# The small products for 1/rms and weight stand in one row in every group of experts

## The chip, the cores and the metric

The kernel runs on one core of one Trainium2 chip. The metric is the device time of one execution in microseconds (us); less is better. TensorE (PE in the rows) multiplies, VectorE (DVE), ScalarE (ACT) and GpSimd (POOL) work element by element, and SyncE (SP) issues all transfers from HBM in one queue.

## What is computed

A block of two models on 256 tokens of 1024 features: sparse attention, a mixture of experts, a gated embedding, a second attention with a second mixture of experts and gated embedding, and then a feed-forward part, a mixer and another feed-forward part. The change touches the two mixtures alone. Cut to what matters:

```python
def hier_moe(xn, w_group, b_group, w_expert, b_expert, w_gate, w_up, w_down):
    ...
    e_w, e_idx = lax.top_k(e_prob, TOPK_IN_GROUP)     # 2 of 8 experts in one of 4 groups
    e_w = e_w / jnp.sum(e_w, axis=-1, keepdims=True)
    comb = g_w * e_w
    ...
    hid = jax.nn.silu(jnp.einsum('td,edf->tef', xt, w_gate)) * jnp.einsum('td,edf->tef', xt, w_up)
    y = jnp.einsum('tef,efd->td', hid * cw[:, :, None], w_down)
```

Each token goes to 2 of 32 experts (`w_gate`, `w_up`: 1024 x 128 each, `w_down`: 128 x 1024). The input `xn` is normalised, so each token has a factor 1/rms as well as its two weights.

## The kernel before

The experts are worked through in four groups of eight (`gq` 0 to 3). Each expert has 32 slots, so a group has 256 slots, in two halves of 128 (`pp` 0 and 1; a half is four experts). For a group the kernel does this:

- `slots` (L1018 and after, on VectorE): for each of two tiles of tokens `t` it makes matrices of zeros and ones that say which token sits in which slot: `G1[t][:, 0]` for a token's first expert, `G[:, t]` for both. `slots_second` makes `G1[t][:, 1]`, for the second expert (on GpSimd in groups 1 to 3).
- `gather` (L1063, TensorE): 32 products with `G` bring the tokens into slots, each with a moving operand of 256 columns over the whole 128 x 128 array.
- `gate_up` (L1086, TensorE): for each half 32 products, called with `u` 0 to 3, eight each. A product uses 32 columns of the array (`128*32` in the rows), and the four experts `x` of a half use the four groups of 32 columns, so that four products can be under way side by side. In the trace each of these fp32 products is two instructions; a half is therefore 64.
- `slot_values` (L1044, TensorE): eight small products with `G1` as the stationary 128 x 128 operand and four moving columns `rw` (1/rms and weight of each token, each in two parts). They give each slot its 1/rms and weight in a PSUM tile. VectorE then makes `sv` (L1049) and `rr` (L1053, L1054) of it. The function is a generator: each `next` issues one product, the ninth issues the VectorE part.
- `finish` (L1117 to L1132): SiLU with `rr`, the down product L1128, scaling with `sv`. `combine` (L1234) adds the result to the tokens. The last group's own version of these is `last_group` (down products L1175).

In groups 0 to 2 the small products are issued by `gate_up` of the second half, one after every second product of it (`x % K["svx"] == 0`, with `svx` 2):

```python
if beside and x % K["svx"] == 0:
    next(beside, None)
```

In group 3 `last_group` begins with `list(values)`, which issues all eight at once. What follows a half's products in groups 0 to 2 is `slots` of the next group, which writes into the two `G1` buffers that the small products of this group read (the pool has two), and then its `gather`.

Loads: the gate and up weights (`in_moe_gu`, 1 MB each, L282) and the down weights (`in_moe_dn`, 512 KB each, tile `wd`, L1102) are issued on SP's queue as soon as the buffers that they go to were read by the products of an earlier group. A scheduler with priorities decides the order of instructions on each engine. In the second mixture one expert has more tokens than slots, and a branch after `combine` of group 1 works through it as a whole (L1418 to L1477); in the first the branch is passed over.

Of the kernel before, what the change touches and what calls it, by code (L numbers as in the profile page):

```python
# [23 lines left out]
K = dict(  # L24
    raw=9,
    e=7,
    w4=5,
    load_at=[1, 1],
    over_at=1,
    defer=0,  # L30
    kinds='rwwrererrrrwrr',
    mid='e',
# [17 lines left out]
    split_first=1,  # L50
    w1_early=1,
    sv=1,
    svx=2,
    fill={'nsa:0': [2, 0], 'nsa:3': [3], 'ffn:0': [6, 7], 'mixer:0': [12, 13], 'ffn:2': [16], 'moba:3': [8, 4], 'nsa:5': [5], 'ffn0:2': [17, 15], 'nsa:2': [9, 14, 1], 'nsa:7': [10], 'ffn0:3': [11]})
FF_GROUPS = [4, 4, 4, 4, 4, 2]
Z_WIDTHS = [512, 512, 304, 256, 512, 512]
# [140 lines left out]
class Block:  # L197
# [63 lines left out]
    def inline(self, ins, line="tail"):  # L261

        self.tc.stamp_issue_order_token(ins.ins, line)
        return ins
# [699 lines left out]
    def moe(self, i, aT, w_out):  # L964
# [9 lines left out]
        def pump(kind):  # L974

            if hold:
                held.append(kind)
            elif pending:
                load(*pending.pop(0), dict(r="raw", e="e", w="w4")[kind])
# [92 lines left out]
        def gather(gq, k):  # L1072
            ps = self.psb([P, 2, 256])
            for t in range(2):
                gather_tile(gq, k, ps, t)

        def gate_up(gq, pp, u, beside=None, bank=None):
            _, _, xg, pgs, _ = st[gq]
            if u == 0:
                pgs.append((bank or self.psa)([P, 2, P]))  # L1080
            where, wg = ahead.pop((gq, pp, u))
            for kk in range(2):
                k = 2 * u + kk
                for x in range(4):
                    o = pp * P + 32 * x
                    mm = nc.tensor.matmul(pgs[pp][32 * x:32 * x + 32], xg[:, k, o:o + 32], wg[kk][:, x],  # L1086
                                          start=(k == 0), stop=(k == KT - 1))
                    if gq == 3 and pp:
                        inline(mm)
                    if beside and x % K["svx"] == 0:  # L1090
                        next(beside, None)
            if where == "raw" and kept and (gq, pp, u) >= kept[0]:
                kept.clear()
            elif where == "raw" or where == "e" and K["recycle"]:
                pump(where[0])
# [87 lines left out]
        def combine_half(back, n):  # L1183
            for t in range(2):
                ps = self.psa([P, 512])
                for b, (GT, y) in enumerate(back):
                    inline(nc.tensor.matmul(ps, GT[:, t * P:(t + 1) * P], y[:, n * 512:(n + 1) * 512],  # L1187
                                            start=(b == 0), stop=(b == len(back) - 1)))
                inline(self.add_h(n, t, ps))

        def last_group(back, values):

            list(values)
            first_hidden = hidden(3, 0)
            next(first_hidden)
            gate_up(3, 1, 0, None, self.psb)
            gate_up(3, 1, 1)
            hT = next(first_hidden)
            combine_half(back, 0)
            gate_up(3, 1, 2)  # L1200
            combine_half(back, 1)
            GT = [token_parts(pp) for pp in range(2)]
            gate_up(3, 1, 3)
            y = [down_products(3, 0, wd[3, 0], hT)]
            self.fine = bool(K["fine"])
            self.gate_first = [list(self.halves(self.unit("w_gate", i * D * D, 2048), 2048, 4))]
            second_hidden = hidden(3, 1)
            next(second_hidden)
            acc = [[self.psa([P, 512]) for _ in range(2)] for _ in range(2)]

            def gathered(pp, n, t):
                for part in range(2):
                    inline(nc.tensor.matmul(acc[t][n], GT[pp][:, t * P:(t + 1) * P], y[pp][part][:, n * 512:(n + 1) * 512],
                                            start=(pp + part == 0), stop=(pp + part == 2)))

            with self.ahead_by("finish"):
                for n in range(2):
                    gathered(0, n, 0)
                hT = next(second_hidden)
                for n in range(2):  # L1220
                    gathered(0, n, 1)
                y.append(down_products(3, 1, wd[3, 1], hT))
                for t in range(2):
                    for n in range(2):
                        gathered(1, n, t)
                        inline(self.add_h(n, t, acc[t][n]))
# [34 lines left out]
        def load_down(gq, pp):  # L1261
            wd[gq, pp] = weights_down(8 * i + 2 * gq + pp)
# [59 lines left out]
        def point(gq, j):  # L1322
            if not K["defer"] and [gq, j] == list(K["load_at"]):
                over_n.append(self.overflow_load(i, n_full, first))

        for gq in range(4):
            if K["defer"] and gq == K["over_at"]:
                hold.append(1)
            values = slot_values(gq)
            if gq == 3:  # L1330
                last_group(back, values)
                break
            if K["svx"] == 0:
                list(values)
            point(gq, 0)
            for u in range(4):
                gate_up(gq, 1, u, values if K["svx"] else None)
            list(values)
            point(gq, 1)
            slots_start(gq + 1)  # L1340
            slots(gq + 1)
            for k in range(4):
                gather(gq + 1, k)
            back = finish(gq, 0, wd[gq, 0])
            if not hold:
                load_down(gq + 1, 0)
            for u in range(4):
                gate_up(gq + 1, 0, u)
            back = back + finish(gq, 1, wd[gq, 1])
            point(gq, 2)  # L1350
            if not hold:
                load_down(gq + 1, 1)
            point(gq, 3)
            if gq == 2:
                continue
            combine(back)
            if gq == K["over_at"]:
                if K["defer"]:
                    over_n.append(self.overflow_load(i, n_full, first, False))
                self.overflow(i, xh, r, w, OH, over, full, over_n[0], first, xT if K["keep"][i] else None)  # L1360
                if not hold:
                    pump("r")
                if hold:
                    hold.clear()
                    for kind in held[:4]:
                        pump(kind)
                    if gq < 3:
                        for pp in range(2):
                            load_down(gq + 1, pp)
                    for kind in held[4:]:  # L1370
                        pump(kind)
# [425 lines left out]
```

## Time and profile before

| | |
|---|---|
| median of 3 runs | 1105.34 us (1105.32 to 1106.97) |
| the profiled execution | 1107.02 us, of which the span of its instructions 1105.0 us |
| mean granted TensorE clock | 0.985 of full |
| busy: PE, DVE, ACT, POOL | 1056.6, 688.9, 517.9, 21.5 us |
| moved by DMA | 268.53 MB, mean 243 GB/s |

The span is the time from the first to the last instruction of the profiled execution. All times in rows count from its start. The first mixture lies at about 205 to 315 us, the second at about 445 to 572 us. A column `PEclk` of 1.00 is the full clock of TensorE (2.4 GHz), 0.5 is the half (1.2 GHz); a value between is a stretch with both.

### The profile page before, as it was taken

The page shows a single profiled execution, that of the slowest core. Times are in us where ns is not written, and L with a number is a line of the kernel's source. Part 1 is how long each engine was busy: PE and PEld are TensorE (multiplying, and loading weights), DVE is VectorE, ACT ScalarE, POOL GpSimd, SP SyncE. Part 2 cuts the span into 40 slices and gives each one's busy share as a digit, 9 for nine tenths or more (in the row PEclk, how much of TensorE's full clock was granted, in tenths as well). Part 3 has the DMA queues.
Part 4 walks back from the last instruction along what each step waited for, and adds up shares of the span by engine and source line. Part 5 has one row for each costly group of instructions (what it writes and reads, how often), then busy time and mean ns, then how long its engine had stood idle before and what let it go on. Part 6 is the DMA issues. An engine that isn't in the chain of part 4 may idle for free.

```text
span 1105.0 us, 18061 instructions
## 1 busy us (share of the span) xinstructions
PE 1056.6 (96%) x6941; PEld 819.6 (74%) x6941; DVE 688.9 (62%) x1730; ACT 517.9 (47%) x1015; POOL 21.5 (2%) x31
## 2 busy tenths in 40 slices
PE   7999999899999999999998999999989989999996
PEld 5885556765557657667556899899969768999995
DVE  6687684643478954644368756565684876555555
ACT  5356575222267675123156543443554755444442
POOL 2000000000100000000000000000000000000000
PEclk9998999899999999899999999999999999999999
DMA  9664568689994485799797656755574354554401
GB/s 371 277 232 193 239 252 324 242 309 383 415 416 174 168 336 182 276 350 380 279 390 279 251 188 210 287 190 181 211 317 178 121 223 153 190 191 153 144 29 38
DMA packets 46506, 268.53 MB, mean 243 GB/s; under 512 B 5328, under 2 KB 7120, under 8 KB 20432
## 3 DMA queue, kind: packets, MB, share of 16 engines
q1 hardware_dynamic: 46416, 267.34, 64.0%
q8 instruction: 56, 0.92, 0.3%
q14 instruction: 34, 0.28, 0.1%
HBM read 266.27 MB, written 1.05 MB: 242 GB/s over the span
## 4 chain that ended last, share of the span: by engine, by line
PE 46%; DVE 3%; ACT 1%; issue 1%; DVEq 0%
PE b L312 7%; PE b L313 7%; PE b L314 7%; PE a L312 6%; PE a L313 6%; PE a L314 6%; PE a L1086 1%; DVE lo L300 1%; PE b L1568 1%; DVE w L1590 1%; DVE h L1591 0%; PE b L1063 0%; PE a L1187 0%; ACT hi L299 0%; DVE nq L327 0%
## 5 line engine op out<-in xcount | busy, mean ns | idle before, releaser
L300 DVE TENSOR_TENSOR lo<-raw,hi 128x1024 fp32r<-128x1024 f32 (+2 forms) x234 | 271.6, 1164 | 189.2 <-ACT hi L299 184.8
L299 ACT ACTIVATE hi<-raw 128x1024 fp32r<-128x1024 f32 (+2 forms) x234 | 235.6, 1011 | 253.1 <-PE b L313 125.6
L312 PE MATMUL a<-hi,e 128*128 128x512 f32 (+2 forms) x576 | 225.2, 392 | 2.5 <-ACT e L399 1.7
L313 PE MATMUL a<-lo,e 128*128 128x512 f32 (+2 forms) x576 | 223.0, 388 | 0.9 <-DVE lo L300 0.9
L314 PE MATMUL a<-hi,e 128*128 128x512 f32 (+2 forms) x576 | 223.0, 388 | 0.0
L312 PE MATMUL b<-e,hi 128*128 128x256 f32 x640 | 181.5, 284 | 0.0
L313 PE MATMUL b<-e,hi 128*128 128x256 f32 x640 | 181.1, 283 | 0.0
L314 PE MATMUL b<-e,lo 128*128 128x256 f32 x640 | 180.9, 283 | 0.0
L312 PEld LDWEIGHTS a<-hi,e 128*128 128x128 f32 x576 | 109.2, 190 | 25.3 <-ACT e L399 2.8
L313 PEld LDWEIGHTS a<-lo,e 128*128 128x128 f32 x576 | 109.1, 189 | 22.6 <-DVE lo L300 2.1
L314 PEld LDWEIGHTS a<-hi,e 128*128 128x128 f32 x576 | 108.7, 189 | 22.0 <-DVE e L389 0.4
L312 PEld LDWEIGHTS b<-e,hi 128*128 128x128 f32 x640 | 122.8, 192 | 1.1 <-ACT hi L299 0.8
L313 PEld LDWEIGHTS b<-e,hi 128*128 128x128 f32 x640 | 122.8, 192 | 0.3
L314 PEld LDWEIGHTS b<-e,lo 128*128 128x128 f32 x640 | 122.8, 192 | 0.0
L1086 PE MATMUL a<-raw,e 128*32 128x256 f32 x704 | 66.1, 387 | 1.1 <-DVEq L1404 0.8
L591 ACT ACTIVATE p<-p,m 128x128 f32<-128x128 f32 (+1 forms) x96 | 42.8, 449 | 13.4 <-DVE m L586 11.4
L336 ACT ACTIVATE junk<-h 128x512 bf16<-128x512 f32 x40 | 25.4, 643 | 37.5 <-DVE h L496 21.9
L1086 PEld LDWEIGHTS a<-raw,e 128*32 128x32 f32 x704 | 27.5, 110 | 15.1 <-issue 2.5
L1063 PE MATMUL b<-G,e 128*128 128x256 f32 x224 | 35.8, 307 | 2.4 <-DVE e L1246 2.3
L586 DVE CUSTOM_DVE_ANT_0 p<-a,consts 128x128 f32<-128x128 f32 (+1 forms) x96 | 31.8, 350 | 10.0 <-PE a L579 3.2
L496 DVE TENSOR_TENSOR h<-h,a 128x512 f32<-128x512 f32 x40 | 26.8, 685 | 16.3 <-PE a L1187 6.6
L269 ACT ACTIVATE e<-b,small 128x256 f32<-128x256 f32 x32 | 15.2, 476 | 44.4 <-DVE e L271 44.2
(339 smaller groups left out, 1373.1 us busy)
## 6 DMA issues: line engine op xcount, KB each, us to landing
raw<-in_ffn SPq DMA_DIRECT2D x62, 1024.0 KB, 4.8
raw<-in_moe_gu SPq DMA_DIRECT2D x52, 1024.0 KB, 7.6
raw<-in_w_ada SPq DMA_DIRECT2D x36, 1024.0 KB, 5.8
wd<-in_moe_dn SPq DMA_DIRECT2D x64, 512.0 KB, 7.1
raw<-in_w_gate SPq DMA_DIRECT2D x8, 1024.0 KB, 13.0
raw<-in_w_m_in SPq DMA_DIRECT2D x8, 1024.0 KB, 6.3
raw<-in_w_a_in SPq DMA_DIRECT2D x7, 1024.0 KB, 10.9
e<-in_moe_gu SPq DMA_DIRECT2D x6, 1024.0 KB, 6.8
```

Of the source, the lines that this page charges most:

```text
L269: self.nc.scalar.activation(out, in_, AF.Identity, scale=scale)
L299: nc.scalar.activation(hi[:, sl], raw[:, at], AF.Copy)
L300: eng.tensor_tensor(lo[:, sl], raw[:, at], hi[:, sl], op=OP.subtract)
L312: mm(out, l[0], r[0], start=start, stop=False, **kw)
L313: mm(out, l[0], r[1], start=False, stop=False, **kw)
L314: mm(out, l[1], r[0], start=False, stop=stop, **kw)
L336: self.nc.scalar.activation(junk, self.h[:, t, half * 512:(half + 1) * 512], AF.Square, accum_out=out)
L496: return self.nc.vector.tensor_tensor(self.h[:, t, sl], self.h[:, t, sl], ps, op=OP.add)
L586: nc.vector.tensor_tensor_reduce(out=p, in0=s, in1=dist[:, a:b], scale=-float(slopes[2 * j + i % 2]), scalar=3e38, op0=OP.add, op1=OP.min, ...
L591: nc.scalar.activation(p, p, AF.Exp, bias=m[:, i:i + 1], scale=-1.0, accum_out=den[:, i:i + 1])
L1063: mm = nc.tensor.matmul(ps[:, j], xh[part][:, t, sl], G[:, t], start=(t + j + part == 0), stop=(t + part == 2), skip_group_check=True)
L1086: mm = nc.tensor.matmul(pgs[pp][32 * x:32 * x + 32], xg[:, k, o:o + 32], wg[kk][:, x], start=(k == 0), stop=(k == KT - 1))
```

## The change

The products no longer stand between those of `gate_up`. In groups 1 and 2 all eight are issued in one row ahead of the second half's `gate_up`, in group 0 in one row behind it, in group 3 as before. The number of instructions on each engine stays the same.

```diff
@@ K
-    svx=2,
@@ gate_up
-        def gate_up(gq, pp, u, beside=None, bank=None):
+        def gate_up(gq, pp, u, bank=None):
...
                     if gq == 3 and pp:
                         inline(mm)
-                    if beside and x % K["svx"] == 0:
-                        next(beside, None)
@@ last_group
-            gate_up(3, 1, 0, None, self.psb)
+            gate_up(3, 1, 0, self.psb)
@@ for gq in range(4)
-            if K["svx"] == 0:
+            if gq:
                 list(values)
             point(gq, 0)
             for u in range(4):
-                gate_up(gq, 1, u, values if K["svx"] else None)
+                gate_up(gq, 1, u)
             list(values)
```

Line numbers of the changed kernel are one less up to `slot_values` (L1044 is L1043), and three less behind `gate_up` (L1128 is L1125). In the rows below a `G_2039` or the like is one of the `G1` tiles, `a` and `b` are PSUM tiles, `e` holds the gathered tokens; a count x8 is eight products of the program.

TensorE in group 0 of the first mixture, end of the first half and the second half, before:

```order
L1086 MATMUL a<-raw,e 32x256 x8
L1086 MATMUL a<-e 32x256
L1044 MATMUL b<-rw,G_2039 128x4
L1086 MATMUL a<-e 32x256 x2
L1044 MATMUL b<-rw,G_2039 128x4
L1086 MATMUL a<-e 32x256 x2
L1044 MATMUL b<-rw,G_2040 128x4
```

The second half of the same group, up to the gather of group 1, in the changed kernel:

```order
L1085 MATMUL a<-raw,e 32x256 x8
L1085 MATMUL a<-e 32x256 x8
L1085 MATMUL a<-raw,e 32x256 x8
L1043 MATMUL b<-rw,G_2039 128x4 x2
L1043 MATMUL b<-rw,G_2040 128x4 x2
L1043 MATMUL b<-rw,G_2039 128x4 x2
L1043 MATMUL b<-rw,G_2040 128x4 x2
L1062 MATMUL b<-G,e 128x256 x25
```

The eight small products moved behind the whole half, directly ahead of the gather of group 1.

VectorE at the same place, where it writes `G1` (two tiles) and `G` of group 1, before:

```order
L1022 TENSOR_SCALAR G_2384<-consts,slg 128x256
L1023 SCALAR_TENSOR_TENSOR G<-consts,slg,G_2384 128x256
L1049 TENSOR_REDUCE sv<-b 128x4
L1022 TENSOR_SCALAR G_2385<-consts,slg 128x256
L1053 TENSOR_SCALAR rr<-sv 128x2
L1023 SCALAR_TENSOR_TENSOR G<-consts,slg,G_2385 128x256
L1054 TENSOR_TENSOR rr<-sv,rr 128x2
```

And in the changed kernel:

```order
L1021 TENSOR_SCALAR G_2384<-consts,slg 128x256
L1048 TENSOR_REDUCE sv<-b 128x4
L1022 SCALAR_TENSOR_TENSOR G<-consts,slg,G_2384 128x256
L1052 TENSOR_SCALAR rr<-sv 128x2
L1021 TENSOR_SCALAR G_2385<-consts,slg 128x256
L1053 TENSOR_TENSOR rr<-sv,rr 128x2
L1022 SCALAR_TENSOR_TENSOR G<-consts,slg,G_2385 128x256
```

The reduction of the small products' result now stands ahead of the first write of `G`.

TensorE at the beginning of the second half of group 1, behind `combine`, in the changed kernel (before, this place reads like group 0, one small product after every second one of L1086):

```order
L1231 MATMUL a<-w_2525,GT 128x512
L1043 MATMUL b<-rw,G_2384 128x4 x2
L1043 MATMUL b<-rw,G_2385 128x4 x2
L1043 MATMUL b<-rw,G_2384 128x4 x2
L1043 MATMUL b<-rw,G_2385 128x4 x2
L1085 MATMUL a<-raw,e 32x256 x16
L1085 MATMUL a<-e 32x256 x8
L1085 MATMUL a<-raw,e 32x256 x8
L1062 MATMUL b<-G,e 128x256 x25
```

Here the row moved ahead of the half, and 32 products without a break lie between it and the gather of group 2.

## Rows read from the trace of the kernel before

**Rows 1.** The page, part 1: busy us, share of the span, instructions of TensorE.

```profile
PE 1056.6 (96%) x6941; PEld 819.6 (74%) x6941; DVE 688.9 (62%) x1730; ACT 517.9 (47%) x1015; POOL 21.5 (2%) x31
```

**Rows 2.** Line L1044, the small products: ns min/median/max; last row: who waited, us, times.

```profile
L1044 PEld LDWEIGHTS b<-rw,G x64: 186/186/192, 223.9 to 550.0; 128*128 128x128 f32 x64
L1044 PE MATMUL b<-rw,G x64: 243/272/272, 223.9 to 550.0; 128*128 128x4 f32 x64
...
  DVE G L1022: 27.0, 6
```

**Rows 3.** Timeline of TensorE, group 0 of the first mixture: start us, us, what.

```profile
223.34 0.59 PE L1086 MATMUL a<-e 128*32 128x256 f32 x2
223.87 0.27 PE L1044 MATMUL b<-rw,G 128*128 128x4 f32 x1
...
224.63 0.27 PE L1044 MATMUL b<-rw,G 128*128 128x4 f32 x1
...
231.65 1.58 PE L1063 MATMUL b<-G,e 128*128 128x256 f32 x11
```

**Rows 4.** Timeline of TensorE, group 3 of the second mixture.

```profile
547.32 1.93 PE L1086 MATMUL a<-raw,e 128*32 128x256 f32 x32
549.18 1.05 PE L1044 MATMUL b<-rw,G 128*128 128x4 f32 x8
...
551.92 1.04 PE L1128 MATMUL a<-wd,hT 128*32 128x512 f32 x8
```

**Rows 5.** Timeline of TensorE, groups 1 to 3 of the first mixture.

```profile
248.06 0.62 PE L1086 MATMUL a<-raw,e 128*32 128x256 f32 x2
...
256.39 3.26 PE L1063 MATMUL b<-G,e 128*128 128x256 f32 x25
...
273.39 0.62 PE L1086 MATMUL a<-raw,e 128*32 128x256 f32 x2 [0.84 <-DVEq L1404]
...
281.90 3.26 PE L1063 MATMUL b<-G,e 128*128 128x256 f32 x25
...
304.54 1.90 PE L1175 MATMUL b<-wd,hT 128*32 128x512 f32 x16
```

**Rows 6.** Timeline of VectorE, writes of the slot matrices for group 1, first mixture.

```profile
227.97 0.35 DVE L1022 TENSOR_SCALAR G<-consts,slg 128x256 fp32r<-128x256 f32 x1 [4.91 <-PE b L1044]
228.36 0.48 DVE L1023 SCALAR_TENSOR_TENSOR G<-consts,slg,G 128x256 fp32r<-128x256 f32 x1
229.48 0.17 DVE L1049 TENSOR_REDUCE sv<-b 128x4 f32<-128x8 f32 x1 [0.64 <-PE b L1044]
...
229.95 0.48 DVE L1023 SCALAR_TENSOR_TENSOR G<-consts,slg,G 128x256 fp32r<-128x256 f32 x1
```

**Rows 7.** Stretches: us, busy of PE, PEld, DVE, ACT, POOL, then PEclk, DMA share, GB/s.

```profile
210.00:215.00 5.00, 3.30 (x20) 2.98 (x20) 4.72 (x32) 0.00 (x0) 0.00 (x0) 0.73 1.00 400
235.00:240.00 5.00, 5.00 (x43) 2.38 (x45) 2.85 (x6) 3.46 (x9) 0.00 (x0) 1.00 0.79 295
260.00:265.00 5.00, 5.00 (x50) 2.39 (x53) 1.17 (x4) 2.46 (x8) 0.00 (x0) 1.00 0.80 303
270.00:275.00 5.00, 4.03 (x20) 2.37 (x18) 2.84 (x5) 0.00 (x0) 0.00 (x0) 1.00 0.97 354
285.00:290.00 5.00, 5.00 (x55) 2.60 (x57) 2.96 (x6) 3.58 (x10) 0.00 (x0) 1.00 1.03 427
335.00:340.00 5.00, 5.00 (x24) 4.14 (x23) 3.69 (x5) 5.00 (x10) 0.00 (x0) 1.00 0.25 102
530.00:535.00 5.00, 4.60 (x22) 1.61 (x20) 2.24 (x3) 0.00 (x0) 0.00 (x0) 1.00 0.39 135
```

**Rows 8.** Waits of SP's queue, 200 to 345 us: us in total, times, longest.

```profile
SPq L1102 <- PE a L1128: 17.4, 6, 5.0
```

**Rows 9.** Timeline of SP: the fourth down-weight load of group 3, first half, first mixture.

```profile
288.68 0.38 SPq L1102 DMA_DIRECT2D wd<-in_moe_dn  x1
```

**Rows 10.** DMA view of that one issue: KB, us from issue to landing.

```profile
wd<-in_moe_dn SPq DMA_DIRECT2D x1, 512.0 KB, 13.4
```

## Prediction

> **What bounds the kernel now.** I read the page first: TensorE is busy for 96% of the span [rows 1], so what shortens its work shortens the kernel, unless something else then comes last. Next I read the line of the small products: there are 64 (two mixtures, four groups, eight each), each some 0.27 us long with a weight load of 0.19 us, and VectorE waited 27.0 us in six places for them before it could write the next group's slot matrices [rows 2]. Busy time says little here, as matmuls overlap. So I took from the timeline of TensorE where the work after each half starts, and let the differences of starts speak. At the end I read the transfers of the first mixture, because they run at their full rate there.
>
> **What an interleaved small product costs.** In group 0 the first small product starts at 223.87 and the next at 224.63 [rows 3]. Between them stand four instructions of L1086 (two products). So one small product with its four instructions takes 0.76 us. In group 3, where nothing is put between, 32 instructions of L1086 take from 547.32 to 549.18, or 1.86 us [rows 4], four of them 0.23 us. The rest, 0.53 us, is the price of one small product among column-group products: the narrow ones have to run out before a full-width one starts, only two of the four column groups are filled at a time, and the narrow ones start anew behind it. In the row of group 3, eight take 1.05 us including the 0.27 us of the last one, so they start 0.11 us apart [rows 2, 4].
>
> **What a half costs before and after.** Start of the half to start of the gather: 223.34 to 231.65 in group 0 is 8.31 us [rows 3]; 248.06 to 256.39 in group 1 is 8.33 us; 273.39 to 281.90 in group 2 is 8.51 us [rows 5]. The same 64 + 8 instructions with the eight in one row stand in group 3 of the second mixture, from 547.32 to 551.92, which is 4.60 us [rows 4]. There the row lies in the middle, in the change at an end; it has one change from narrow to full width and back in either case, so I take 4.60 for all. This gives back 3.71, 3.73 and 3.91 us. Nothing hides these, as TensorE has no wait of its own in them.
>
> **What the change adds: a wait in group 0.** VectorE may write the first `G1` tile of group 1 when the small products have read it, and the first `G` after that. Now this is done under the 17 products of the half that follow the last small one. After the change the gather comes right behind the row. Its sixth product is the last to read the first tile; it ends 5 x 0.11 + 0.27 = 0.83 us after the row's start. VectorE starts 0.04 us later, its second write 0.39 us after its first (227.97 to 228.36), and that takes 0.48 us [rows 6]: the first `G` is there at 1.74 us. (The reduction that now stands between them fits: it can start at 1.09, when all eight are done, and takes 0.08 us of VectorE's time beside the 0.39.) TensorE is through with the row at 8 x 0.11 = 0.89 us. It waits 0.85 us. Queued behind the waiting gather are the other products of it and the down products, so the wait is TensorE's own. Seven gather products need only the first tile; they take 7 x 0.12 us (25 start within 3.26 us [rows 5]), which covers most of the second tile's write. The bounds: 0, if the wait were hidden, and 2.4 us, if all products needed both tiles: 0.87 + (229.95 + 0.48 - 227.97) - 0.89 [rows 6]. I take 0.85, since the order lets the first tile's products go first. In groups 1 and 2 the row stands ahead of the 64 instructions, some 3.5 us of cover for the same writes, so I cost it at nothing there. Should that cover fail, it would be 0.85 us each.
>
> The other moves cost nothing that I see: `sv` and `rr` come later in group 0, but they are first needed by the SiLU of `finish`, behind 25 gather products (3.1 us); GpSimd's part is needed a group later.
>
> TensorE's own account for one mixture: 3.71 - 0.85 + 3.73 + 3.91 = 10.5 us.
>
> **Where a part of it is lost: the transfers of the first mixture.** They run at 427 GB/s at 285 us [rows 7]. The fourth down-weight load of group 3's first half is issued at 288.68 and lands 13.4 us later, at 302.1 [rows 9, 10]. TensorE needs it for the second half of L1175, 304.54 + 0.95 = 305.5 [rows 5]. So it has 3.4 us to spare, and TensorE wants to come 10.5 us earlier. How much earlier can the load land? Loads are held back by products that free their buffers: down weights waited six times, 17.4 us, for L1128 [rows 8]. So the stream moves with TensorE where it isn't full: at 235 to 240 us it carries 295 GB/s [rows 7], so the gain of group 0, 3.71 - 0.85 = 2.9 us, is passed on. Behind that, two dips close when their loads come early: (427 - 303) x 5 / 427 = 1.45 us and (427 - 354) x 5 / 427 = 0.85 us [rows 7]. The load lands 2.9 + 2.3 = 5.2 us earlier, and the first mixture gains 3.4 + 5.2 = 8.6 us instead of 10.5. Bounds: 3.4 us if the stream doesn't move, 10.5 if it moves freely. I take 8.6, as the releases are seen in the waits. By 335 to 340 us the stream is down to 102 GB/s [rows 7], so the backlog has ended before the next stage needs its weights.
>
> In the second mixture the expert with too many tokens lies between, and the stream falls to 135 GB/s at 530 to 535 us [rows 7]; the loads after it are held by TensorE alone and come earlier with it. The second mixture repeats the pattern of the first: 10.5 us.
>
> **Sum.** 8.6 + 10.5 = 19.1 us. The profiled execution took 1107.02 us, 1.68 above the median of the three timed runs, and becomes 1087.9, its span 1085.9; the median of 1105.34 becomes 1086.2.
>
> **A rule that speaks against it.** The eight in the row took 1.05 us in group 3 [rows 4]; one by one, each with its load of 0.19 and its product of 0.27 us, they would be 8 x 0.46 = 3.7 us [rows 2]. The Trainium skill (TensorE: Matmul & The Clock Gate, section Part 3: Packing small matmuls — row/col tiling) says that a weight load overlaps with matmuls under way only when it goes to another row group; these eight all use every row, so by that rule the loads would lie open in the row, and the sum would be 4.8 us. The trace disagrees in that one row of eight.
>
> **The rivals.**
> - *The transfers don't move* (20%). The first mixture gains only 3.4 us, in all 13.9, which gives 1091.4. For it: the stream is full at 285 us. Against: the dips, and the waits for L1128 [rows 7, 8]. It would show as waits of L1125's or L1172's products for `wd`.
> - *The loads of the row lie open* (4%). A row of eight takes 3.7 us, 2.7 more: 6 x 2.7 = 16 us less for TensorE. Then the first mixture wants 10.5 - 8.1 = 2.4 us, under the 3.4 to spare, and both give 4.8: 1100.5. Against: [rows 4].
> - *Slower: the clock falls* (3%). TensorE ran partly at the 1.2 GHz level at 210 to 215 us (0.73), after waits, when it was busy for 3.30 of 5 us [rows 7]. If the wait in front of the gather, or eight products with four columns each, brought it there for each half, 4.60 us would be 9.2: 0.9, 0.9 and 0.7 us more than now and the 0.85 on top, 3.3 us a mixture, 1112. It decides from 80% of these stretches at 1.2 GHz on (4.60 x 1.8 = 8.3). Against: the 0.84 us wait at 272 us [rows 5] left 270 to 275 us at 1.00 [rows 7].
> - *No change* (2%): several of the losses together. That the change doesn't do what it says is out: the order of the changed kernel shows the rows of eight in all six groups.
>
> **How the numbers follow.** The forecast has 70%; its own range is 1084 to 1088.5 (at one end both mixtures full, 2 x 10.5 = 21.0 us; at the other the dips half closed, 1.15 us less, and the wait in front of the gather half as long again, 0.4 us twice: 19.1 - 2.0 = 17.1 us). The wide range reaches to the first rival, 1091.4 and some more for a longer wait, and down to a gain of 22.7 (no wait, 2 x 0.85 more than 21.0). I give 1083 to 1092. Some 0.2%, 2.2 us, is what a measurement tells from no change. Faster: 70 + 20 + 4 and the remaining 1, 95%; same 2%; slower 3%.
>
> **What would show it.** In the changed trace: rows of L1043 x8 of about 1 us in eight places; halves of 4.6 us; a wait of L1062 for `G` of L1022 of some 0.85 us in group 0 of each mixture and in no other; L1172 in the first mixture's last group waiting for its weights, 1.9 us, and none in the second; the clock unchanged. Wrong would be: waits of L1062 in groups 1 and 2, a wait for weights of over 4 us in the first mixture, or a later stage that doesn't come earlier by the sum of both.

## The result, and the profile after

The changed kernel takes 1094.38 us (median of 4 runs, 1089.81 to 1096.23) where the kernel before takes 1106.12 beside it: ratio 0.9882, 95% interval 0.9869 to 0.9895. It is faster, as forecast, but by 11.7 us and not by 19.1, and 1094.38 lies outside the range of 1083 to 1092. Two later sets of runs of the same kernel gave 1091.48 and 1090.25 (ratios 0.9867 and 0.9847, below). The profiled execution of this section took 1094.51 us, its span is 1092.7 us.

The page, part 1, as in [rows 1]: TensorE does the same 6941 instructions in 17.0 us less of busy time.

```profile
PE 1039.6 (95%) x6941; PEld 814.9 (75%) x6941; DVE 689.2 (63%) x1730; ACT 517.7 (47%) x1015; POOL 23.1 (2%) x31
```

The small products are now L1043. Who waited for them, us and times, as in [rows 2]:

```profile
  DVE G L1021: 12.3, 4
  DVE sv L1048: 7.1, 2
```

TensorE in group 0 of the first mixture, second half, row and gather (L1062), which answers to [rows 3]:

```profile
225.38 1.05 PE L1085 MATMUL a<-e 128*32 128x256 f32 x16
...
228.94 1.05 PE L1043 MATMUL b<-rw,G 128*128 128x4 f32 x8
230.74 1.09 PE L1062 MATMUL b<-G,e 128*128 128x256 f32 x7 [0.75 <-DVE G L1022]
232.08 2.17 PE L1062 MATMUL b<-G,e 128*128 128x256 f32 x16 [0.24 <-DVE G L1022]
```

The half with its row takes 228.94 + 0.89 - 225.38 = 4.45 us, and the gather waits for `G` twice: 0.75 us for the first tile, and, seven products later, 0.24 us for the second.

Groups 1 and 2 of the first mixture, which answer to [rows 5]:

```profile
247.58 0.95 PE L1043 MATMUL b<-rw,G 128*128 128x4 f32 x8
...
252.04 1.21 PE L1062 MATMUL b<-G,e 128*128 128x256 f32 x8
...
269.04 0.62 PE L1085 MATMUL a<-raw,e 128*32 128x256 f32 x2 [0.84 <-DVEq L1401]
269.79 1.02 PE L1043 MATMUL b<-rw,G 128*128 128x4 f32 x8
270.75 3.96 PE L1085 MATMUL a<-raw,e 128*32 128x256 f32 x62
274.64 1.57 PE L1062 MATMUL b<-G,e 128*128 128x256 f32 x11
```

Group 1 is as forecast: 252.04 - 247.58 = 4.46 us. In group 2 the scheduler put one product of L1085 (two instructions) ahead of the row, so the width changes once more there: 274.64 - 269.04 = 5.60 us.

The last group of the first mixture, and the start of the next stage (L403). Before, L1175 at 304.54 had no wait in front of it [rows 5]:

```profile
289.42 1.07 PE L1085 MATMUL b<-raw,e 128*32 128x256 f32 x16 [0.30 <-DMA raw<-in_moe_gu]
291.90 1.07 PE L1085 MATMUL b<-raw,e 128*32 128x256 f32 x16 [1.41 <-DMA raw<-in_moe_gu]
...
300.80 2.22 PE L1172 MATMUL b<-wd,hT 128*32 128x512 f32 x8 [0.32 <-DMA wd<-in_moe_dn]
...
311.21 1.03 PE L403 MATMUL b<-consts,h 128*128 128x128 f32 x8
```

TensorE now waits for the weights in three places there, and the eight products at 300.80 take 2.22 us instead of some 1.05, as their weights come in one by one.

The stretches of [rows 7] in the changed kernel (columns as there):

```profile
235.00:240.00 5.00, 5.00 (x43) 2.17 (x45) 2.53 (x5) 3.50 (x10) 0.00 (x0) 1.00 0.62 215
260.00:265.00 5.00, 5.00 (x77) 3.10 (x67) 2.07 (x3) 2.46 (x5) 0.00 (x0) 1.00 0.94 355
270.00:275.00 5.00, 4.90 (x73) 2.95 (x73) 2.76 (x9) 0.37 (x1) 1.49 (x2) 1.00 0.96 329
285.00:290.00 5.00, 4.70 (x45) 2.18 (x45) 1.74 (x7) 1.74 (x3) 0.00 (x0) 1.00 1.02 423
```

Of the two dips that the prediction closed, one is half closed (303 to 355 GB/s), the other deeper than before (354 to 329), and at 235 us there is less than before (295 to 215). These windows lie at equal times from the start of the span; the half in group 0 starts 2.04 us later in this execution. At an equal distance from its start the two dips carry 320 and 364 GB/s here (first two rows), and in a second profile of the same kernel (last two rows; the first experiment below) 408 and 410:

```profile
262.04:267.04 5.00, 5.00 (x48) 3.35 (x41) 2.93 (x5) 0.79 (x2) 0.00 (x0) 1.00 0.87 320
272.04:277.04 5.00, 4.90 (x62) 3.45 (x55) 2.10 (x6) 0.50 (x2) 1.21 (x2) 1.00 0.98 364
261.27:266.27 5.00, 5.00 (x48) 3.35 (x41) 2.93 (x5) 0.77 (x2) 0.00 (x0) 1.00 1.02 408
271.27:276.27 5.00, 5.00 (x64) 3.89 (x57) 2.37 (x6) 0.47 (x1) 1.18 (x2) 1.00 0.99 410
```

What SyncE's queue waited for, 200 to 345 us, as in [rows 8] (us in total, times, longest):

```profile
SPq L1390 <- SPq L1390: 9.1, 7, 2.5
SPq L1099 <- DMA raw<-in_moe_gu: 8.4, 4, 2.1
...
SPq L1099 <- PE a L1125: 7.6, 2, 7.2
...
SPq L1423 <- SPq L1423: 5.4, 5, 1.4
```

The wait for TensorE's down products is down from 17.4 to 7.6 us, and that for the gate and up products (L282, here L281) from 24.2 to 10.9. Two others stand in its place: waits for loads that are still under way, and waits of SyncE at L1390 and L1423, the two places of the branch that the first mixture passes over. In the kernel before, the same two lines had 3.2 us each:

```profile
SPq L1426 <- SPq L1426: 3.2, 3, 2.2
SPq L1393 <- SPq L1393: 3.2, 3, 2.5
```

The trace shows what is waited for at L1390: six of the seven waits, 8.9 of the 9.1 us, end within 0.05 us of the landing of a load that was issued before. The last of these loads, of `raw`, is issued at 245.17 and lands 15.3 us later, at 260.47; the next load leaves SyncE at 260.94.

The load of [rows 9] and [rows 10], in the timeline of SyncE and in the DMA view:

```profile
286.96 0.33 SPq L1099 DMA_DIRECT2D wd<-in_moe_dn  x1
```

```profile
wd<-in_moe_dn SPq DMA_DIRECT2D x1, 512.0 KB, 15.0
```

It is issued 1.7 us earlier than before and needs 1.6 us longer, so it lands at 301.96, practically where it landed before.

The second mixture, start of the half in group 0, row of group 1, second half of group 2, and next stage:

```profile
460.36 1.05 PE L1085 MATMUL a<-e 128*32 128x256 f32 x16
...
482.55 0.95 PE L1043 MATMUL b<-rw,G 128*128 128x4 f32 x8
...
522.86 0.59 PE L1085 MATMUL a<-raw,e 128*32 128x256 f32 x2 [0.30 <-PEq L1423]
...
559.75 1.47 PE L403 MATMUL b<-consts,h 128*128 128x128 f32 x12
```

### The profile page after: what moved, and what is told of

It is laid out like the page before. It is cut to its first block, busy times and chain, and to the rows that moved or that the text cites. A ratio compares the mean times of both kernels' runs of the same rounds, so it can differ in the third digit from the quotient of the medians.

```text
span 1092.7 us, 18059 instructions
## 1 busy us (share of the span) xinstructions
PE 1039.6 (95%) x6941; PEld 814.9 (75%) x6941; DVE 689.2 (63%) x1730; ACT 517.7 (47%) x1015; POOL 23.1 (2%) x31
## 3 DMA queue, kind: packets, MB, share of 16 engines
HBM read 266.27 MB, written 1.05 MB: 245 GB/s over the span
## 4 chain that ended last, share of the span: by engine, by line
PE 44%; DVE 4%; DMA 2%; ACT 1%; issue 1%; DVEq 0%; ACTq 0%
PE b L311 7%; PE b L313 7%; PE b L312 7%; PE a L311 6%; PE a L312 6%; PE a L313 6%; DMA raw<-in_w_ada 2%; DVE lo L299 1%; PE a L1085 1%; PE b L1565 1%; DVE w L1587 1%; PE a L1549 0%; DVE h L1588 0%; ACT hi L298 0%; PE b L1062 0%
## 5 line engine op out<-in xcount | busy, mean ns | idle before, releaser
L590 ACT ACTIVATE p<-p,m 128x128 f32<-128x128 f32 (+1 forms) x96 | 42.8, 449 | 13.5 <-DVE m L585 11.5
L1085 PE MATMUL a<-raw,e 128*32 128x256 f32 x704 | 47.2, 385 | 1.2 <-DVEq L1401 0.8
L1062 PE MATMUL b<-G,e 128*128 128x256 f32 x224 | 36.0, 306 | 4.4 <-DVE e L1243 2.3
L1085 PEld LDWEIGHTS a<-raw,e 128*32 128x32 f32 x704 | 25.1, 111 | 17.1 <-issue 3.3
L268 ACT ACTIVATE e<-b,small 128x256 f32<-128x256 f32 x32 | 15.2, 476 | 47.1 <-DVE e L270 46.8
```

The costliest lines, as they stand in the source:

```text
L268: self.nc.scalar.activation(out, in_, AF.Identity, scale=scale)
L590: nc.scalar.activation(p, p, AF.Exp, bias=m[:, i:i + 1], scale=-1.0, accum_out=den[:, i:i + 1])
L1062: mm = nc.tensor.matmul(ps[:, j], xh[part][:, t, sl], G[:, t], start=(t + j + part == 0), stop=(t + part == 2), skip_group_check=True)
```

## The experiments

A mixture is measured in all kernels from the start of group 0's second half (or of the row ahead of it) to the first product of the next stage, in the timeline of TensorE of the profiled execution; "less" is against the kernel before.

| kernel | mixture 1: from, to | less | mixture 2: from, to | less |
|---|---|---|---|---|
| before | 223.34, 314.64 | | 463.09, 572.07 | |
| changed (above) | 225.38, 311.21 | 5.47 | 460.36, 559.75 | 9.59 |
| changed, again | 224.61, 308.41 | 7.50 | 456.93, 556.12 | 9.79 |
| changed, again 2 | 221.77, 307.62 | 5.45 | 457.01, 556.38 | 9.61 |
| row ahead in all | 223.67, 307.33 | 7.64 | 456.30, 554.37 | 10.91 |
| row ahead, again | 223.26, 307.41 | 7.15 | 456.05, 554.11 | 10.92 |
| changed, no branch | 223.06, 306.56 | 7.80 | 455.39, 554.75 | 9.62 |
| before, no branch | 223.33, 312.91 | 1.72 | 462.20, 571.16 | 0.02 |
| changed, lighter stream | 222.26, 303.20 | 10.36 | (other work) | |
| every fourth | 225.42, 311.86 | 4.86 | 460.66, 564.76 | 4.88 |
| rows in mixture 1 only | 224.11, 307.81 | 7.60 | 456.66, 565.67 | -0.03 |
| rows in mixture 2 only | 224.62, 315.92 | 0.00 | 464.12, 561.79 | 11.31 |
| row ahead of the combine | 222.11, 306.58 | 6.83 | 455.02, 557.85 | 6.15 |
| before, shifted | 224.13, 316.33 | -0.90 | 464.48, 574.16 | -0.70 |

### The changed kernel twice more

No edit.

> The changed kernel once more, to see how far its runs lie apart and with which granted clock. If the 12 us are the change's own, all runs stand at 1093 to 1096 us and the clock explains nothing. If stretches at 1.2 GHz that fall here or there take a part of the gain, runs with a mean clock of 0.985 stand near 1090 us and runs with 0.980 near 1095 us: 0.001 of the clock is 1.1 us at the low level and so about 1.1 us of time.

> The changed kernel once more. The gain of the two mixtures is 17 us (7.5 and 9.7); what the time shows of it depends on the granted clock: 1090 at 0.985, 1091.5 at 0.983, 1094.5 at 0.980. Rival: the gain of the first mixture itself varies (5.5 in one execution, 7.5 in another), and the time doesn't follow the clock.

Measured: 1091.48 us (1090.02 to 1094.39, 5 runs; before beside it 1106.75), ratio 0.9867 [0.9851, 0.9884]; and 1090.25 us (1089.02 to 1095.14, 6 runs; before 1106.95), ratio 0.9847 [0.9834, 0.9860]. Each run comes with its mean granted clock. The 15 runs of the changed kernel, and 46 of the kernel before that stood beside the experiments:

| mean granted clock | before, us | changed, us |
|---|---|---|
| 0.987 | 11 runs, 1104.75 to 1105.94 | none |
| 0.985 | 19 runs, 1105.84 to 1107.53 | 5 runs, 1089.02 to 1090.02 |
| 0.984 | 16 runs, 1106.59 to 1109.27 | 1 run, 1094.51 |
| 0.983 | none | 5 runs, 1090.94 to 1091.57 |
| 0.979 to 0.981 | none | 4 runs, 1094.25 to 1096.23 |

At 0.985 the medians are 1106.31 and 1089.55: 16.8 us, which is the 15 to 17 us that the two mixtures are shorter in the table above. Over all runs it is 1106.41 to 1091.18, 15.2 us. So the first set of four had two runs at the lowest clocks in it. From 0.985 to 0.980 the changed kernel goes from 1089.55 to 1094.32 (median of two), about 1 us for 0.001. The time doesn't follow the clock alone: the run of 1094.51 at 0.984 is slower than all five at 0.983. It is the first profile, and the gain of its first mixture is 5.5 us; that gain varies as well, 5.5 or 7.5 us.

### The row ahead of the half in group 0 too

```diff
 (against the kernel before)
-    svx=2,
+    svx=0,
```

> The row stands ahead of the second half in group 0 too. If the wait for the slot matrices in group 0 is what the row's place costs there, both waits in front of and inside the gather (0.75 and 0.24 us, with what lies around them some 1.3 us) go in both mixtures: in the second it is 1.3 us less at its end, in the first less than that, as its last group waits for weights. In all 1.3 to 2.6 us less than the changed kernel. If the row has to wait for the four columns that it multiplies (made shortly before), the wait only changes its place and the time is the same within 0.3 us.

> The kernel with the row ahead of the second half in group 0 too, once more. Theory: the second mixture gains 10.9 us (1.3 more than in the changed kernel, since no gather waits for G), the first is held by its weights at 5.5 to 8; 1088.5 at a granted clock of 0.985, 1090 at 0.983. Rival (it is no better than the changed kernel, 1089.0 to 1090.0 at 0.985): the 1.3 us of the second mixture don't reach the end.

Measured: 1089.61 us (1085.49 to 1091.59), ratio 0.9841 [0.9820, 0.9861]; again 1088.61 (1085.80 to 1090.62), ratio 0.9832 [0.9813, 0.9851]. The timeline of TensorE (second profile) has no wait in front of the gather (L1063 here):

```profile
223.26 1.05 PE L1044 MATMUL b<-rw,G 128*128 128x4 f32 x8
224.25 1.07 PE L1086 MATMUL a<-e 128*32 128x256 f32 x16
...
227.84 0.39 PE L1063 MATMUL b<-G,e 128*128 128x256 f32 x1
```

227.84 - 223.26 = 4.58 us. So the two waits of the changed kernel cost 1.3 us a mixture: 10.9 against 9.6 to 9.8 in the second. In the first the 1.3 us can't be seen beside the 2 us by which executions differ. At a clock of 0.983 its two runs took 1089.61 and 1089.70, the changed kernel's five 1090.94 to 1091.57. It is the fastest version here, though the intervals of the ratios overlap.

### Without the branch that the first mixture passes over

```diff
 (overflow_load; overflow likewise returns at once where i is 0)
-        n = self.nc.values_load(n_full[0:1, 0:1], min_val=0, max_val=32)
+        n = self.nc.values_load(n_full[0:1, 0:1], min_val=0, max_val=32) if i else None
...
+        if not i:
+            return None
```

This leaves out the work of a crowded expert in the first mixture, of which there is none in this input. The same edit was made to the changed kernel and to the kernel before.

> The changed kernel without the two branches of the first mixture (the ones that are passed over there). Theory: at the end of each branch SP's queue waits until every load issued before has landed, so the dips of the stream behind group 1 can't close, and the first mixture's last group waits for weights. Then without the branches the first mixture gains 2.5 to 4 us on the changed kernel: 1 us for the jump on TensorE, the rest from waits for weights that go. Rival: the stream runs at its full rate and the branches don't matter: then only the jump goes, 0.8 to 1 us, and the waits of L1085 and L1172 for weights stay or grow.

> The kernel before without the same two branches. It has no wait for weights in the last group, so both theories expect 0.8 to 1 us less than before from the jump alone. Compared with the row without branches: if the branches hold the stream, the first mixture now gains some 8.5 to 9.5 us from the row, start of group 0 to the end of the mixture; if the stream's rate is the limit, it gains 6 us as with the branches.

Measured: the changed kernel without it 1090.01 us (1087.85 to 1090.68), ratio 0.9848 [0.9834, 0.9863]; the kernel before without it 1105.98 (1104.79 to 1107.72), ratio 0.9995 [0.9986, 1.0004]. In the former, SyncE's waits at the branch are gone, but those of TensorE for the weights are not:

```profile
284.72 1.07 PE L1085 MATMUL b<-raw,e 128*32 128x256 f32 x16 [1.16 <-DMA raw<-in_moe_gu]
287.20 1.08 PE L1085 MATMUL b<-raw,e 128*32 128x256 f32 x8 [1.41 <-DMA raw<-in_moe_gu]
```

The fourth load of [rows 9] is issued at 282.26 there and takes 15.0 us: it lands at 297.26, 74.2 us after the start of the half in group 0. In the first profile of the changed kernel that is 301.96 - 225.38 = 76.6 us, in the second, with the branch, it is issued at 284.15, takes 15.0 us, and lands after 74.5. So at most 2.4 us go with the branch, and the second execution has its load as early with the branch: it isn't the branch that makes the weights come last. From one kernel without the branch to the other, the first mixture gets 89.58 - 83.50 = 6.1 us shorter. That is what was expected if the rate of the stream is the limit (6), and not if the branches hold it (8.5 to 9.5). The kernel before is 1.72 us shorter in the first mixture without it, and not in the time: its 11 runs have clocks of 0.981 to 0.985, those of before 0.984 to 0.987.

### A lighter stream

```diff
 (against the changed kernel, load_down)
+            if i == 0 and (gq, pp) == (2, 1):
+                wd[gq, pp] = wd[2, 0]
+                return
```

> The changed kernel without four of the down-weight loads of the first mixture (2 MB; the second half of group 2 uses the weights of the first half there, so the output of the mixture is another). Theory (in the first mixture the stream of weights runs at its full rate and comes last): 2 MB at 427 GB/s are 4.9 us of stream, so the waits of group 3's gate_up and down products for raw and wd (1.7 and 0.3 us in the changed kernel) go, and the first mixture is 1.7 to 3 us shorter: 1088.5 to 1090 where the changed kernel takes 1091.5. Rival (what holds the loads is SyncE's wait at the end of the passed-over branches, and not the rate): the loads behind the branches leave SyncE at the same time, the waits stay between 1.5 and 2 us and the time stays at 1091.5.

Measured: 1076.47 us (1075.49 to 1077.76). The time can't be used: with the other output of the first mixture the second has no crowded expert, and TensorE does 6867 instructions instead of 6941. The first mixture can be read by itself. All that TensorE waited for between 280 and 304 us (us, times, longest):

```profile
PE a L1210 <- DVE w L1177: 0.6, 2, 0.3
PE b L1157 <- DVE hb L1153: 0.2, 1, 0.2
```

The two waits that are left are in the kernel before as well; those for `raw` and `wd` are gone. SyncE's waits at the two places of the branch are still there, 8.6 and 5.0 us (9.1 and 5.4 in the changed kernel), so it isn't these that made the weights late. The mixture is 10.36 us shorter than before, 0.78 of it because the scheduler ordered group 3 otherwise (a whole row there, 6.61 us instead of 7.39 from one half to the next). The other 9.6 are what the second mixture gains. That speaks for the theory: with the stream relieved, the first mixture gives what the second gives.

### One small product after every fourth

```diff
 (against the kernel before)
-    svx=2,
+    svx=4,
```

> The kernel before with one small product after every fourth column-group product instead of every second. Theory A (half of the price of 0.53 us comes from only two of the four column groups being filled between two small products): a half takes 8.3 - 8 x 0.27 = 6.2 us; the last small product now stands near the end of the half, so each gather waits some 0.5 us for G, six times 3 us; in all 6 x 2.1 - 3 = 9.6 us less, 1097. Theory B (the whole price is the run-out and new start at each change of width): the half stays at 8.3 us and the waits add 3 us: 1109.7.

Measured: 1100.23 us (1098.83 to 1104.82; before 1106.04), ratio 0.9949 [0.9930, 0.9967], at clocks of 0.978 to 0.983. TensorE in group 0:

```profile
225.94 0.27 PE L1044 MATMUL b<-rw,G 128*128 128x4 f32 x1
226.15 0.64 PE L1086 MATMUL a<-e 128*32 128x256 f32 x8
226.72 0.27 PE L1044 MATMUL b<-rw,G 128*128 128x4 f32 x1
...
232.10 3.26 PE L1063 MATMUL b<-G,e 128*128 128x256 f32 x25
```

One small product with eight instructions takes 0.78 us, which leaves 0.78 - 8 x 1.86 / 32 = 0.31 us for it (32 instructions take 1.86 us, [rows 4]), against 0.53 with four. So nearly half of the price came from the half-filled column groups: theory A. The half in group 0 takes 232.10 - 225.42 = 6.7 us instead of 8.3, and three times 1.6 is the 4.9 us of each mixture. The two mixtures are 9.7 us shorter together, as theory A had it (9.6); the time is only 5.8 us less, at the lower clocks. The waits for `G` that were expected don't come: the first tile's last reader stands two products earlier, and the gather starts without a wait.

### The rows in one mixture alone

```diff
 (against the kernel before; == 1 for the other run)
-            if K["svx"] == 0:
+            if gq and i == 0:
...
-                gate_up(gq, 1, u, values if K["svx"] else None)
+                gate_up(gq, 1, u, values if i != 0 else None)
```

> The rows of the change in the first mixture alone; the second mixture as before. Theory (the first mixture gives less, because its weights come last): 6 to 7.5 us less than before, 1099.2 to 1100.7. Rival (both mixtures give the same and the loss lies elsewhere, in the clock): 8.2 us less, half of the whole, 1098.5, and no wait of TensorE for raw or wd in the last group.

> The rows of the change in the second mixture alone. Theory: 9 to 9.6 us less than before, 1097.1 to 1097.7 (10.5 as predicted, less 0.65 for the product that the scheduler puts ahead of the row in group 2 and 0.25 for the second wait for G in group 0). Rival (a gain in the second mixture is partly given back in the stages behind it, at 590 to 800 us): under 7.5 us.

Measured: rows in the first mixture alone 1101.46 us (1098.58 to 1104.18), ratio 0.9957 [0.9941, 0.9973]; in the second alone 1099.54 (1095.30 to 1100.05), ratio 0.9932 [0.9915, 0.9950]; before beside them 1106.04. So 4.6 and 6.5 us in the time where the mixtures are 7.6 and 11.3 us shorter (1.7 of the 11.3 because a stretch at 1.2 GHz that the profile of before has at 526 to 530 us isn't there). Both have clocks of 0.979 to 0.987 in their runs, on the average 0.982 and 0.983, where before beside them has 0.9855. The first mixture gives less than the second, as the theory has it, and neither shows in full: both medians lie above the times that the theory gave (1100.7 and 1097.7 at most). The 6.5 us of the second would also fit its rival (under 7.5, a part given back in the stages behind). In its profile these stages take 0.9 us more than before (1095.6 - 561.79 against 1105.0 - 572.07), so the rival isn't ruled out.

### The kernel before, shifted by less than a microsecond

```diff
             if gq == 3:
+                list(slot_values(gq))
+                values = slot_values(gq)
                 last_group(back, values)
```

> The kernel before with the row of eight in group 3 issued twice in both mixtures, so that all behind it comes 0.9 and then 1.8 us later; nothing else is changed. Theory (the time that TensorE spends at 1.2 GHz elsewhere is larger in every kernel whose times are shifted against before, by rows or otherwise): granted clock 0.983 instead of 0.985, time 1106.4 + 1.8 + 2 = 1110. Rival (it is the rows that bring the lower clock): clock 0.985, time 1108.2.

Measured: 1111.30 us (1109.73 to 1113.43), ratio 1.0038 [1.0024, 1.0051]; before 1106.95. The mixtures are 0.9 and 0.7 us longer, the time 4.35 us (2.7 to 5.6). The clock of its runs is 0.979 to 0.983, of before 0.984 to 0.985. There is no row in groups 0 to 2 here, so the lower clock comes without these rows too.

### The row ahead of the combine

```diff
 (against the changed kernel)
-            values = slot_values(gq)
+            values = early.pop(gq, None) or slot_values(gq)
...
-            if gq:
-                list(values)
+            list(values)
...
-            list(values)
...
             if gq == 2:
                 continue
+            early[gq + 1] = slot_values(gq + 1)
+            list(early[gq + 1])
             combine(back)
```

> The small products of groups 1 and 2 in a row ahead of the combine of the group before (between column-group products and full-width ones), those of group 0 ahead of its second half. Theory (each change of width costs, the product that the scheduler puts ahead of the row in group 2 costs 0.65 us, and in the first mixture the stream of weights comes last): no product ahead of a row and one change of width less in groups 1 and 2; the second mixture gains 11.5 to 12 us against before (9.7 in the changed kernel, 10.9 with the row ahead in all groups), the first still 7.5 to 8: 1088.5, 1 us below the row ahead in all. Rival (the row's place doesn't matter as long as it is a row): the second mixture gains 10.9 or less, 1089.6.

Measured: 1096.78 us (1095.78 to 1097.49), ratio 0.9909 [0.9894, 0.9924], with a clock of 0.976 in all four runs. In group 2 TensorE waits behind the row. The timeline of TensorE, that of VectorE, and the stretch behind the wait:

```profile
258.93 1.05 PE L1043 MATMUL b<-rw,G 128*128 128x4 f32 x8
262.76 1.94 PE L1125 MATMUL a<-wd,hT 128*32 128x512 f32 x8 [2.77 <-issue]
264.62 5.86 PE L1231 MATMUL a<-w,GT 128*128 128x512 f32 x16
```

```profile
259.87 0.35 DVE L1021 TENSOR_SCALAR G<-consts,slg 128x256 fp32r<-128x256 f32 x1 [4.82 <-PE b L1043]
...
262.31 0.35 DVE L1116 SCALAR_TENSOR_TENSOR hb<-hb,rr,a 128x128 f32<-128x128 f32 x1
```

```profile
265.00:270.00 5.00, 5.00 (x15) 3.96 (x15) 2.78 (x5) 0.46 (x1) 0.00 (x0) 0.62 1.00 395
```

VectorE stands idle for 4.82 us until the row is done, then works on the slot matrices, `sv` and `rr`, and only behind these writes `hb` of the SiLU (262.31 + 0.35). TensorE's down products start 0.1 us after that. So the row, put this early, holds up the SiLU of the group before. Behind the wait of 2.77 us the clock is partly at 1.2 GHz: L1231 takes 5.86 us where it takes 3.9 in the other kernels. The second mixture has the same place with 2.63 and 5.57 us. Its gain is 6.15 us, not the 11.5 to 12 of the theory nor the 10.9 of its rival. What one change of width less is worth isn't tested by this, as the wait covers it.

## Why the prediction was wrong

Two steps make up most of the miss. The last load of the first mixture (step 3) came 2.2 or 4.2 us earlier and not 5.2, and that mixture gave 1.1 to 3.1 us less than forecast. The clock (step 4) was costed at nothing and took most of the rest: the mixtures alone, 15.1 to 17.3 us shorter, would have brought 1106.4 to some 1089 to 1091, within the range.

**The price of the small products was right.** Whole rows of eight take 0.95 to 1.05 us, in seven of the eight places; in group 3 of the first mixture the scheduler puts one small product ahead of four down products and seven behind them, as it did before. The half of group 1 takes 4.46 us (forecast 4.60), and the kernel with every fourth shows from the other side what the price is made of. The Trainium skill (TensorE: Matmul & The Clock Gate, section Part 3: Packing small matmuls — row/col tiling) lets a weight load overlap with matmuls under way only where it goes to another row group, by which the loads in a row would lie open and a row would take 3.7 us. No whole row here takes more than 1.05 us, so the traces disagree.

**Step 1, the wait in group 0: mis-sized.** Forecast 0.85 us; the first wait is 0.75 (the gather starts 1.80 us after the row, forecast 1.74), but the second tile's write, which I took to be covered by seven products, comes 0.24 us after them, and from the first of the seven to the eighth are 1.34 us instead of 0.84. Counted from the start of the half, the gather ends 0.4 us later than forecast in each mixture. Moving the row ahead removes all of it (10.9 instead of 9.6).

**Step 2, group 2: mis-sized.** I took 4.60 us for it. With one product ahead of the row it is 5.60 in the first profile and 5.24 in the second mixture (528.10 - 522.86), so the gain is 2.9 us there and 3.2 here (before 540.41 - 531.97 = 8.44), not 3.91. The product ahead stands in the kernel before too (273.39, [rows 5]); there it shows only as 8.51 against 8.33 us, since the width changed all the time anyway. TensorE's account for one mixture is 9.6 to 9.8 us, as the second mixture shows, and not 10.5: 0.4 from step 1, 0.7 from here, and 0.1 back from group 1.

**Step 3, the transfers of the first mixture: the step that failed most.** Its form held: slack 3.4 us, and to that what the load comes earlier. But the load comes, counted from the start of the half in group 0, 78.7 us after it before (288.68 + 13.4 - 223.34) and 76.6 after the change: 2.2 us earlier, and not 5.2. 3.4 + 2.2 = 5.6, and the mixture gave 5.5. The same sum holds in the second profile (74.5: 3.4 + 4.2 = 7.6, and it gave 7.5) and without the branch (74.2: 7.9, and 7.8), so what was wrong is how much earlier the load comes. The gain of group 0 that is passed on is 2.5 us and not 2.9 (step 1): the next load of `wd` leaves 11.26 us after the start of the half, before 13.73. And two dips were to close because their loads are no longer held by TensorE. In the first profile they hardly do (at an equal distance from the half 303 to 320 and 354 to 364 GB/s), in the second they do (408 and 410), in the third, which gave 5.5, one does in part (373 and 347). TensorE does hold them less (SyncE's wait for the down products went down by 9.8 us), but waits for loads under way came instead, those at the branch among them. The lighter stream shows it from the other side. The rival that the transfers don't move is half right; between the two, the executions give 5.5 to 7.5 us. Where one execution of the same kernel gets 2 us less than another can be seen: the last load that SyncE waits for at L1390 takes 15.3 us in the first profile and 13.9 in the second, with the same issues ahead of it, and the first load behind the branch leaves 35.6 us after the start of the half in the first and third profile and 33.9 in the second. Why the load lands later isn't settled.

**Step 4, the clock: taken as unchanged.** The mixtures are 15.1 to 17.3 us shorter in the three profiles, the medians of the three sets 11.7, 15.3 and 16.7, and at an equal clock of 0.985 it is 16.8. Outside the mixtures the three profiles differ from that of before as follows (us more than before). In brackets stands what PEclk gives for the same part: (1 - PEclk) x 10, summed over windows of 10 us, against before.

| part of the span | first profile | second | third |
|---|---|---|---|
| up to the first mixture | 2.04 (1.7) | 1.27 (1.7) | -1.57 (-1.7) |
| between the mixtures | 0.70 (0) | 0.07 (0) | 0.94 (1.7) |
| behind the second | 0.02 (0) | -0.05 (0) | 3.69 (5.1) |

So most of what lies between the mixtures' gain and the time goes with stretches at 1.2 GHz far from the change, at places where the profile of before has none. Three of them follow, from the first and the third profile of the changed kernel and from the shifted one; the number behind the counts is PEclk, and (1 - 0.83) x 10 = 1.7 us, or (1 - 0.66) x 15 = 5.1 us, is what the lower clock takes where TensorE is busy throughout, and less where it isn't:

```profile
130.00:140.00 10.00, 10.00 (x57) 6.88 (x55) 5.38 (x31) 5.38 (x19) 0.00 (x0) 0.83 0.69 283
```

```profile
885.00:900.00 15.00, 12.19 (x45) 7.19 (x46) 11.61 (x46) 5.88 (x17) 0.00 (x0) 0.66 0.78 272
```

```profile
903.00:913.00 10.00, 6.27 (x35) 2.88 (x34) 8.24 (x32) 4.08 (x11) 0.00 (x0) 0.83 0.87 306
```

The forecast's rival had the clock fall in the halves themselves; it didn't, a half of 4.46 us leaves no room for it. The shifted kernel shows that an edit which makes each mixture 0.7 to 0.9 us longer is enough to change the clock elsewhere. What decides where a stretch falls is open; the runs show only that the kernel before has the highest mean clock of all kernels here (0.985 over 46 runs, the others 0.976 to 0.984).

**The sum.** 19.1 forecast, less 0.7 to 0.9 (steps 1 and 2, second mixture), less 1.1 to 3.1 (steps 1 to 3, first mixture), gives 15.1 to 17.3. The medians of the three sets, 11.7 to 16.7, lie at or below this, and how far goes with the clock of their runs.

## What to carry to other kernels

Products of different widths belong apart: here a full-width product among 32-column ones costs 0.3 us even where all four column groups are filled, and 0.5 where two are; and where a row of them frees a buffer that the next step needs, its place is ahead of the long work, not behind it; but not so early that another engine's work queues up behind the row (2.77 us ahead of the combine). A gain on TensorE in a stage whose loads run at full rate is worth the slack of the last load and what that load really moves; count the waits of the issuing queue by what they would wait for next, not only by what they wait for now. Compare times of this kind at an equal granted clock, since here an edit that makes the two mixtures 1.6 us longer together moved the time by 4.35 us (2.7 to 5.6); in its profile 2.9 us of this lie behind the mixtures, where two stretches at 1.2 GHz are new.

## What the runs showed of the hardware that was not expected

A branch that is passed over still costs SyncE time: in the changed kernel its queue stood 9.1 and 5.4 us at L1390 and L1423. At L1390 six of the seven waits ended with the landing of a load issued before, and no load was issued from 250.78 to 260.94 us, while TensorE itself waited only 0.84 us there. A wait of TensorE of 2.77 us was followed by a stretch at 1.2 GHz in which 16 products took 5.86 us instead of 3.9, while the waits of 0.75 and of 0.30 and 1.41 us in the changed kernel were not. Without the branch, where these last two were 1.16 and 1.41, a stretch at 1.2 GHz followed them too (PEclk 0.66 from 286 to 291 us); the products for `wd` didn't come later by it, since their weights landed only at 297. And the same program, run again, had its low stretches in other places: at 130 to 140 us in the first profile of the changed kernel (0.83), not in its third, which had one at 885 to 900 us (0.66).
